# Layer 1's gated MLP: its up projection as a stage of its own with seven block products for eight, and the result through DRAM

## The chip, the cores and the metric

One core of a Trainium2 chip runs the whole program in one launch. The metric is the device time of one execution in microseconds (us). Engines: TensorE (PE; its weight loads are PEld), VectorE (DVE), ScalarE (ACT), GpSimd (POOL) and SyncE (SP), whose queue issues every DMA of this kernel.

## The reference

Two decoder layers over 1024 tokens of width 1024 in float32. Each is attention, a read of a small memory, an output projection added to x, and a gated MLP with a causal convolution, added to x; a final norm follows. The change concerns the MLP of layer 1:

```python
def rmsnorm(x, g):
    y = xf * lax.rsqrt(jnp.mean(xf * xf, axis=-1, keepdims=True) + EPS)
    return (y * g.astype(jnp.float32)).astype(x.dtype)

def conv_glu_ffn(h, w_up, conv_w, conv_b, w_down):      # h = rmsnorm(x, g_ffn): 1024 x 1024
    S = h.shape[1]
    a, b = jnp.split(h @ w_up, 2, axis=-1)              # each 1024 tokens x 2816
    a_pad = jnp.pad(a, ((0, 0), (CONV_WIDTH - 1, 0), (0, 0)))
    a = sum(conv_w[j] * a_pad[:, j:j + S] for j in range(CONV_WIDTH)) + conv_b
    return (jax.nn.silu(a) * b) @ w_down                # back to width 1024
```

## The kernel before

Everything is feature-major: an activation is [feature on partition, token]. The 1024 tokens go in two halves of 512, the width in 8 slices of 128, the inner width of the MLP in NF = 22 tiles of 128. A float32 product x*y runs as three products of rounded parts, H*H + H*L + L*H, where H is the operand rounded and L the rest (`mm3`, lines 209 to 213, so each product is three matmuls, lines 211, 212 and 213). Both operands are needed as such a pair: ScalarE writes H, GpSimd or VectorE subtracts to get L.

Weights stream through the class `Weights` (lines 60 to 113). A first pass over the program records the order of the units; in the second, `_load` (line 77) issues a DMA of a [128, 1024] unit up to `LOAD` = 5 units ahead, and `_split` makes H on ScalarE (line 88) and L on GpSimd (line 89) up to `SPLIT` = 2 units ahead. All big tiles of SBUF come from one pool of 47 buffers of 4 KB a partition (`t4`, line 140). PSUM has two buffers of 1024 columns (`psS`) and four of 512 (`psB`). Engines run in the order in which the program issues. `tick` (line 177) is called with the length of what was just issued on TensorE; background generators (norms, stores) advance by that credit, so they are woven into the issue order by estimated time. A store to DRAM is issued 4000 ns of that clock after it is asked for (`store`, line 160), or as soon as something of the same key is loaded (`flush`).

The MLP is `ffn` (lines 724 to 824). In layer 1 it takes both halves together. For each inner tile f, `up` multiplies the tile of the a-weights with h of both halves (`proj`, 8 slices x 3 matmuls of 512 columns), `conv` multiplies by the norm's scale (line 736), does the three-tap convolution (737 to 744), the activation (745) and the scale for b (746); then come the b-weights, `gate` multiplies (751) and splits the result (755, 756), which stays in SBUF. h here is x * gain, not yet scaled: `gained` (lines 441 to 449) makes it, for the first half as background work and for the second half in a hook of the output projection, and the scale of the tokens (`scale_of`, with the sums of squares in `fold_in`, lines 346 and 354, and `norm_scale`, lines 360 to 388) may come later, but before the first `conv`. After each pair of tiles, `down` multiplies the results of the pair before it with two units of the down weights and adds 128x1024 blocks of PSUM to x (line 802). x of both halves stays in SBUF. The last two pairs go half by half, and the final norm runs behind them.

Ahead of it stand the output projection's last steps (`outs1[1]` in `run`, line 1665, eight steps of `wout_steps`, line 716), beside which the first half's norm runs as background work.

Of the kernel before, what the change touches and what calls it, by code (L numbers as in the profile page):

```python
# [17 lines left out]
F32 = mybir.dt.float32  # L18
# [22 lines left out]
class _Null:  # L41
    """Stands for every object of a pass that only records the weight order."""
# [17 lines left out]
class Weights:  # L60
    """Streams [128, 1024] weight units: load, then split into H and L."""
# [3 lines left out]
    def __init__(self, t, order):  # L65
        self.t, self.order, self.seen = t, order, []
        self.pos = self.loaded = self.ready = 0
        self.ahead = self.LOAD
        self.raw, self.hl = {}, {}

    def _load(self):
        i = self.loaded
        name, idx = self.order[i]
        src = self.t.a[name][idx]
        raw = self.t.t4(1024)
        w = src.shape[-1]
        self.t.nc.sync.dma_start(raw[:, :w], src)
        self.raw[i] = (raw, w)
        self.loaded += 1

    def _split(self):
        i = self.ready
        while self.loaded <= i:
            self._load()
        nc, t = self.t.nc, self.t
        raw, w = self.raw.pop(i)
        hi, lo = t.t4(1024, dt=R32), t.t4(1024, dt=R32)
        nc.scalar.copy(hi[:, :w], raw[:, :w])  # L88
        nc.gpsimd.tensor_tensor(lo[:, :w], raw[:, :w], hi[:, :w].bitcast(F32), op=OP.subtract)  # L89
        self.hl[i] = (hi, lo)  # L90
        self.ready += 1

# [4 lines left out]
    def pump(self):  # L97
        n = len(self.order)
        self.load(min(n, self.pos + self.ahead))
        while self.ready < min(n, self.pos + self.SPLIT):  # L100
            self._split()

    def get(self, name, idx):
        if self.order is None:
            self.seen.append((name, idx))
            return _Null(), _Null()
        i = self.pos
        assert self.order[i] == (name, idx), (self.order[i], name, idx)
# [7 lines left out]
class Unit:  # L116
    """Two generators: the scores with their softmax, and the values."""
# [12 lines left out]
class Trunk:  # L130
# [12 lines left out]
    N_T4 = 47  # L143
# [65 lines left out]
    def mm3(self, out, a, b, start, stop):  # L209
        mm = self.nc.tensor.matmul  # L210
        mm(out, a[0], b[0], start=start, stop=False)  # L211
        mm(out, a[0], b[1], start=False, stop=False)  # L212
        mm(out, a[1], b[0], start=False, stop=stop)  # L213

    def evac_hl(self, hi, lo, src, scale=1.0):
        """hi + lo = scale * src exactly (scale a power of two)."""
# [8 lines left out]
    def split(self, hi, lo, src):  # L225
        """hi + lo = src exactly."""
# [38 lines left out]
    def scratch(self):  # L265
# [11 lines left out]
        self.kB_d = d.tile([2, 256, T], F32, name="kB_d")  # L277

    def rope_tables(self):
        """cos and sin for the 24 frequencies, [frequency, cos|sin, token] in DRAM."""  # L280
# [28 lines left out]
    def load_table(self, kind, hf):  # L309
        """The rows of the table as the rotated rows of a projection need them."""  # L310
# [81 lines left out]
    def norm_apply(self, rb, x, gain, per, out, pace=2500, ease=False):  # L392
        """Generator; appends the split (x * gain) * rb for the tiles [128, per, n] of x."""
# [9 lines left out]
        for i in range(len(x) + 1):  # L403
            if i < len(x):
# [4 lines left out]
                hs.append(h)  # L409
                yield pace  # L410
# [18 lines left out]
    def norm(self, x, gain, out, wait=0, tail=6000, pace=1000, ease=False):  # L429
        """Generator: the whole norm of a half."""  # L430
# [10 lines left out]
    def gained(self, xp, gain, i, out):  # L441
        """Appends the split x * gain of the i-th tile of x, not yet scaled."""
# [8 lines left out]
    def scale_later(self, acc, box, n=HT, wait=5000, big=False):  # L451
        """Generator: the scale of the tokens, put into box."""
# [3 lines left out]
    def scale_of(self, sqs, box, wait=1000):  # L456
        """Generator: the same from the squares of the tiles of x."""
# [8 lines left out]
    def proj(self, out, unit, h, n0=0, n=HT):  # L466
        """out[128 features, n] += unit^T h over the 8 slices of the model width."""
# [8 lines left out]
    def pair(self, name, j0, h, n0=0):  # L476
        """Two feature tiles of a projection, [128, 2, 512 - n0 tokens]."""
# [5 lines left out]
    def rope_store(self, key, S, tab, n0, scale, dst):  # L483
        """(x1 c - x2 s | x2 c + x1 s) * scale of the pair S, split and stored."""
# [15 lines left out]
    def store_hl(self, key, src, dst, scale=1.0, in_sbuf=False):  # L500
        """Splits src [128, 2 tiles, tokens] and stores H and L to dst(hl, tile)."""
# [70 lines left out]
    def mem_norm(self, eng=None):  # L572
        """Generator: the normed memory, split."""
# [56 lines left out]
    def mem_units(self, slot):  # L630
        """The memory read of a half as two pipeline units and the place of its output."""
# [277 lines left out]
    def a_first(self, raw, rb):  # L909
        """The first product runs along with the loads of x."""  # L910
# [25 lines left out]
    def indexer(self, blks):  # L936
        """Generator: the scores of the blocks' queries over all their keys."""
# [285 lines left out]
    def begin_a(self, att):  # L1223
        """Generator: what of attn_a can run before its pipeline."""
# [9 lines left out]
    def run_a(self, hf, att, x, mem, bm, final):  # L1234
        """Runs the attention; returns the last steps of the output projection."""
# [617 lines left out]
```

## Time and profile before

| | us |
|---|---|
| runs | 2714.73, 2715.31, 2716.74 |
| median | 2715.31 |
| the profiled execution: span | 2714.7 |
| of it TensorE busy | 2524.9 |
| VectorE, ScalarE, GpSimd busy | 1649.5, 1137.0, 1289.1 |
| mean granted clock of TensorE | 0.968 |

The span runs from the first to the last instruction of the profiled execution; no other time of that execution is given, and the fastest of the runs, 2714.73 us, is as long as the span to the digit shown. The granted clock is a share of 2.4 GHz; its other level is 1.2 GHz. A matmul's end in these rows is modelled, and matmuls overlap, so the time from start to start is what counts.

### The profile page before, as it was taken

How to read it: one execution, taken by the hardware profiler on the slowest of the kernel's cores; microseconds unless marked ns; L12 is line 12 of the kernel's file. 1: busy time of each engine (PE TensorE's matmuls, PEld its weight loads, DVE VectorE, ACT ScalarE, POOL GpSimd, SP SyncE). 2: the span in 40 equal slices, each digit the busy share in tenths (PEclk: the TensorE clock that was granted, in tenths of full speed). 3: DMA queues.
4: the chain of work that ended last, by engine and by line, in shares of the span. 5: the costliest groups of instructions: out<-in, count | busy, mean ns of one | idle time of the engine just before them, and what ended most of it. 6: DMA issues, size and time to landing. Idle time of an engine off the chain costs nothing.

```text
span 2714.7 us, 33368 instructions
## 1 busy us (share of the span) xinstructions
PE 2524.9 (93%) x12140; PEld 2107.5 (78%) x12140; DVE 1649.5 (61%) x2867; ACT 1137.0 (42%) x2094; POOL 1289.1 (47%) x883
## 2 busy tenths in 40 slices
PE   6788989989998999989999989999999999999997
PEld 5667767867776889878788878888778888888886
DVE  7798997876679466664653453598743333333335
ACT  4344556644542555433332335588622222222223
POOL 4533343345554643345765555566543333333334
PEclk8899999989998999999999999999999999999998
DMA  5444346322222253322332345632211111111101
GB/s 190 152 146 141 117 140 214 128 75 93 87 85 78 68 192 133 109 93 78 109 104 98 111 131 175 232 102 86 78 47 47 47 55 47 47 53 49 47 24 62
DMA packets 105236, 276.10 MB, mean 102 GB/s; under 512 B 11248, under 2 KB 28144, under 8 KB 105072
## 3 DMA queue, kind: packets, MB, share of 16 engines
q1 hardware_dynamic: 105072, 273.98, 30.9%
q8 instruction: 95, 1.56, 0.2%
q14 instruction: 69, 0.57, 0.1%
HBM read 229.89 MB, written 44.04 MB: 101 GB/s over the span
## 4 chain that ended last, share of the span: by engine, by line
PE 47%; DVE 6%; ACT 2%; issue 1%; POOL 1%; DMA 0%; DVEq 0%; ACTq 0%; POOLq 0%
PE pB L211 9%; PE pB L212 9%; PE pB L213 9%; PE pS L211 6%; PE pS L213 6%; PE pS L212 6%; PE pS L1345 1%; PE pB L1399 1%; PE pB L1384 1%; DVE t L739 1%; DVE t L738 1%; DVE t L407 1%; ACT t L88 0%; DVE t L802 0%; DVE t L354 0%
## 5 line engine op out<-in xcount | busy, mean ns | idle before, releaser
L89 POOL TENSOR_TENSOR t<-t,t 128x1024 fp32r<-128x1024 f32 x324 | 792.6, 2462 | 405.4 <-ACT t L88 324.0
L211 PE MATMUL pB<-t,t 128*128 128x512 f32 (+2 forms) x2128 | 800.3, 376 | 7.7 <-DVE t L716 4.1
L212 PE MATMUL pB<-t,t 128*128 128x512 f32 (+2 forms) x2128 | 797.1, 375 | 10.5 <-DVE t L399 8.7
L213 PE MATMUL pB<-t,t 128*128 128x512 f32 (+2 forms) x2128 | 795.7, 374 | 0.1
L211 PE MATMUL pS<-t,t 128*128 128x512 f32 (+1 forms) x1232 | 491.1, 399 | 56.0 <-DVE t L802 31.3
L213 PE MATMUL pS<-t,t 128*128 128x512 f32 (+1 forms) x1232 | 485.0, 394 | 13.5 <-POOL t L89 13.5
L212 PE MATMUL pS<-t,t 128*128 128x512 f32 (+1 forms) x1232 | 484.3, 393 | 1.6 <-DVE t L448 1.6
L212 PEld LDWEIGHTS pB<-t,t 128*128 128x128 f32 (+1 forms) x2128 | 403.6, 190 | 81.9 <-DVE t L399 9.7
L211 PEld LDWEIGHTS pB<-t,t 128*128 128x128 f32 (+1 forms) x2128 | 403.3, 190 | 79.3 <-DVE t L716 5.0
L213 PEld LDWEIGHTS pB<-t,t 128*128 128x128 f32 (+1 forms) x2128 | 403.2, 189 | 72.7 <-POOL t L89 0.7
L746 POOL TENSOR_TENSOR t<-t,t 128x512 f32<-128x512 f32 x88 | 114.3, 1299 | 510.0 <-ACT t L745 503.4
L88 ACT CAST t<-t 128x1024 fp32r<-128x1024 f32 x324 | 328.7, 1043 | 19.4 <-POOL t L89 9.2
L802 DVE TENSOR_TENSOR t<-t,pS 128x1024 f32<-128x1024 f32 (+1 forms) x180 | 214.4, 1195 | 196.3 <-PE pS L213 196.3
L211 PEld LDWEIGHTS pS<-t,t 128*128 128x128 f32 x1232 | 242.4, 197 | 108.7 <-DVE t L802 35.9
L213 PEld LDWEIGHTS pS<-t,t 128*128 128x128 f32 x1232 | 241.8, 196 | 65.9 <-POOL t L89 18.3
L212 PEld LDWEIGHTS pS<-t,t 128*128 128x128 f32 x1232 | 242.8, 197 | 44.7 <-DVE t L448 2.1
L737 ACT ACTIVATE t<-t,conv 128x512 f32<-128x512 f32 x88 | 71.8, 816 | 456.5 <-DVE t L736 456.5
L756 POOL TENSOR_TENSOR t<-t,t 128x512 fp32r<-128x512 f32 x88 | 116.2, 1321 | 182.7 <-ACT t L755 180.4
L220 DVE TENSOR_TENSOR t<-pB,t 128x512 fp32r<-128x512 f32 (+3 forms) x248 | 149.6, 623 | 84.4 <-ACT t L219 78.8
L736 DVE TENSOR_TENSOR t<-pB,t 128x512 f32<-128x512 f32 x88 | 60.7, 690 | 222.4 <-PE pB L213 210.4
L219 ACT CAST t<-pB 128x512 fp32r<-128x512 f32 (+3 forms) x248 | 126.5, 535 | 149.1 <-PE pB L213 81.5
L751 DVE TENSOR_TENSOR t<-t,pB 128x512 f32<-128x512 f32 x88 | 60.4, 687 | 191.9 <-PE pB L213 133.2
(204 smaller groups left out, 2933.3 us busy)
## 6 DMA issues: line engine op xcount, KB each, us to landing
t<-in_up SPq DMA_DIRECT2D x132, 512.0 KB
t<-in_down SPq DMA_DIRECT2D x66, 512.0 KB
t<-in_a_in SPq DMA_DIRECT2D x42, 512.0 KB
t<-in_b_in SPq DMA_DIRECT2D x28, 512.0 KB
t<-in_a_out SPq DMA_DIRECT2D x20, 512.0 KB
t<-in_b_out SPq DMA_DIRECT2D x20, 512.0 KB
t<-in_x SPq DMA_DIRECT2D x16, 512.0 KB
q_d<-t SPq DMA_DIRECT2D x32, 256.0 KB
```

Source lines behind the costliest of these rows:

```text
L88: nc.scalar.copy(hi[:, :w], raw[:, :w])
L89: nc.gpsimd.tensor_tensor(lo[:, :w], raw[:, :w], hi[:, :w].bitcast(F32), op=OP.subtract)
L211: mm(out, a[0], b[0], start=start, stop=False)
L212: mm(out, a[0], b[1], start=False, stop=False)
L213: mm(out, a[1], b[0], start=False, stop=stop)
L219: nc.scalar.copy(hi, src)
L220: nc.vector.tensor_tensor(lo, src, hi.bitcast(F32), op=OP.subtract)
L736: nc.vector.tensor_tensor(v, a, rb[0], op=OP.mult)
L737: nc.scalar.activation(u, v, AF.Identity, bias=cw[:, 3:4], scale=cw[:, 2:3])
L746: nc.gpsimd.tensor_tensor(v, v, rb[0], op=OP.mult)
L756: nc.gpsimd.tensor_tensor(gl[:, f % 2], u, gh[:, f % 2].bitcast(F32), op=OP.subtract)
L802: nc.vector.tensor_tensor(x[dp][:, :, t], x[dp][:, :, t], S, op=OP.add)
```

## The change

The MLP of layer 0 stays. In layer 1, `ffn` is replaced by `ffn_up` and `ffn_down`.

`ffn_up` runs the whole up projection. Tiles f = 0 and 1 go as before, half by half. For f = 2 to 21 the a- and b-weights of a tile are one 2 x 2 block matrix (a or b; first or second 512 of the width), and h is another (first or second 512 of the width; first or second half of the tokens). Their product is formed by seven block products in place of eight (Winograd's variant of Strassen's scheme): seven left factors, of which four are weights as loaded or intermediate sums of them, are made on VectorE from the two raw units (`_factor`), and each is split into H and L of 512 columns; the right factors are h's blocks b11, b21, b22 and four differences of blocks, made and split once, ahead of the first group (`right_factors`). The sums of the products are formed on VectorE and partly in PSUM, where a second product is added to a bank that has been read out already. A product is `product`: 4 slices of `mm3`. The steps that finish one group stand between the products of the next. Since a sum mixes both halves, h is now scaled before the products (`norm_h0`, `norm_h1`), and the scalings in `conv` fall away. h0 is also stored to DRAM and two blocks at a time loaded back for the differences; x of both halves is stored to DRAM.

The gated result is split as before, but stored to DRAM (`G_d`, one [128, 2, 512] tile for each f and half). `ffn_down` loads it, two tiles for each pair and half, one pair ahead (`fetch`), and x is loaded back at the change of stages. Its matmuls and additions are those of `down`. The pool has 51 buffers in place of 47, taken from a smaller DMA scratch (`dynamic_dma_scratch_size=1024`). While the groups run, splits are made four ahead (`AHEAD`). All docstrings and comments are taken out.

```diff
 class Weights:
     def _split(self):
         i = self.ready
-        while self.loaded <= i:
+        while self.loaded < self.need[i]:
             self._load()
...
+        else:
+            src = self._factor(i)
+            hl = t.t4(2, HT, dt=R32)
+            nc.scalar.copy(hl[:, 0], src)
+            nc.gpsimd.tensor_tensor(hl[:, 1], src, hl[:, 0].bitcast(F32), op=OP.subtract)
+            self.hl[i] = (hl[:, 0], hl[:, 1])
         self.ready += 1
+    def _factor(self, i):
+        g, k, tt = self.group, self.order[i][2], self.t.nc.vector.tensor_tensor
...
+        if k == 1:
+            tt(g["s1"][:, 0], b[:, 0], b[:, 1], op=OP.add)
+            tt(g["s1"][:, 1], g["s1"][:, 0], a[:, 0], op=OP.subtract)
+            return g["s1"][:, 1]
+        if k == 2:
+            return g["s1"][:, 0]
+        if k == 3:
+            return a[:, 1]
+        if k == 4:
+            tt(g["s4"][:, 0], a[:, 0], b[:, 0], op=OP.subtract)
+            return g["s4"][:, 0]
+        if k == 5:
+            tt(g["s4"][:, 1], a[:, 1], g["s1"][:, 1], op=OP.subtract)
+            return g["s4"][:, 1]
...
-    N_T4 = 47
+    N_T4 = 51
...
+    def right_factors(self, hf1, out):
...
+        for j in range(2):
+            b11, b21 = self.t4(2, HT), self.t4(2, HT)
+            for i, b in ((j, b11), (2 + j, b21)):
+                self.load("hf", b, self.hf_d[i])
+            while len(hf1) < 3 + j:
+                yield 500
+            yield 2500
...
+            for k, (x, y) in enumerate(((b12, b11), (b22, t[0]), (b22, b12), (b21, t[1]))):
+                tt(t[k], x, y, op=OP.subtract)
+                yield 1400
+                if late:
+                    late()
+                hi, lo = self.t4(2, HT, dt=R32), self.t4(2, HT, dt=R32)
+                nc.scalar.copy(hi, t[k])
+                eng = nc.vector if k % 2 else nc.gpsimd
+                def late(k=k, hi=hi, lo=lo, eng=eng):
+                    eng.tensor_tensor(lo, t[k], hi.bitcast(F32), op=OP.subtract)
+                    out[k].append((hi, lo))
+                yield 1400
...
+    def product(self, out, a, b, start, tick=True):
+        for s in range(4):
+            ks = slice(s * 128, s * 128 + 128)
+            hp = b[s // 2]
+            self.mm3(out, (a[0][:, ks], a[1][:, ks]), (hp[0][:, s % 2], hp[1][:, s % 2]),
+                     start and s == 0, s == 3, again=not start)
+            if s % 2:
+                self.tick(6 * 222)
+    def ffn_up(self, l, h, ready, B, n_std, near_end):
...
+        def keep(f, hf, u):
+            t = self.t4(2, HT, dt=R32)
+            nc.scalar.copy(t[:, 0], u)
+            nc.gpsimd.tensor_tensor(t[:, 1], u, t[:, 0].bitcast(F32), op=OP.subtract)
+            self.store("G", self.G_d[f][hf], t.bitcast(F32))
...
+        def group(f):
+            S, C = self.psS(), self.psB()
+            A, Bk = S[:, :HT], S[:, HT:]
...
+            mul(A, b11, True)
+            nc.scalar.copy(c1, A)
+            yield
+            mul(Bk, B[1], True)
+            tt(u2, c1, Bk, op=OP.add)
+            yield
+            mul(C, B[0], True)
+            tt(v, c1, C, op=OP.add)
+            yield
+            mul(A, b21, False)
+            ua = conv(f, 0, A)
+            yield
+            mul(Bk, B[2], False)
+            tt(c22, v, Bk, op=OP.add)
+            nc.scalar.activation(ua, ua, AF.Silu)
+            yield
+            mul(C, b22, False)
+            tt(c12, u2, C, op=OP.add)
+            ub = conv(f, 1, c12)
+            yield
+            mul(Bk, B[3], False)
+            tt(c21, c1, Bk, op=OP.add)
+            tt(ua, ua, c21, op=OP.mult)
+            nc.scalar.activation(ub, ub, AF.Silu)
+            yield
+            keep(f, 0, ua)
+            tt(ub, ub, c22, op=OP.mult)
+            yield
+            keep(f, 1, ub)
...
+    AHEAD = 4
+    def ffn_down(self, l, xs, G, fetch, hooks, last):
...
+        for c in range(nch - 2):
+            us = weights(c)
+            for hf in range(2):
+                if c + 1 + hf < nch:
+                    fetch(c + 1, hf)
+                down(c, us, G.pop((c, hf)), hf)
...
-        def early_h0():
-            for i in range(4):
-                self.gained(x0[i], g[:, 4], i, h0)
-                yield 3500
+        def norm_h0():
+            yield from self.norm_apply(rb0[0], x0, g[:, 4], 2, h0, 2500, keep=lambda i, t: self.store("hf", self.hf_d[i], t))
+            yield from self.store_x(x0, self.x_d[0])
+            x0.x = None
+        def norm_h1():
+            yield from self.scale_of(sqs, rb1, 1000)
+            del sqs[:]
+            yield from self.norm_apply(rb1[0], x1, g[:, 4], 2, h1, 2000, keep=lambda i, t: hf1.append(t))
+            yield from self.store_x(x1, self.x_d[1])
+            x1.x = None
...
+        b1 = self.add_bg(norm_h1())
+        bT = self.add_bg(self.right_factors(hf1, B))
...
-        self.ffn(1, [(0, x0, h0, rb0, last0), (1, x1, h1, rb1, last1)], last=1)
+        self.ffn_down(1, xs, G, fetch, [last0, last1], 1)
```

## Rows read from the trace of the kernel before

**Rows 1.** The page's busy times: us, share of the span, instructions.
```profile
PE 2524.9 (93%) x12140; PEld 2107.5 (78%) x12140; DVE 1649.5 (61%) x2867; ACT 1137.0 (42%) x2094; POOL 1289.1 (47%) x883
```

**Rows 2.** Windows: each engine's busy us and count, granted clock, DMA share, GB/s.
```profile
core 0: us, PE busy (x) PEld busy (x) DVE busy (x) ACT busy (x) POOL busy (x), PEclk, DMA share, GB/s
0.00:10.00 10.00, 0.62 (x2) 0.50 (x2) 2.21 (x5) 4.22 (x6) 3.08 (x14) 1.00 0.74 239
10.00:20.00 10.00, 7.14 (x23) 4.87 (x22) 9.72 (x14) 8.87 (x11) 4.16 (x2) 1.00 0.76 302
...
1986.00:1992.00 6.00, 6.00 (x19) 4.77 (x20) 1.96 (x12) 0.00 (x0) 0.00 (x0) 0.55 0.21 81
...
2035.00:2470.00 435.00, 435.00 (x1920) 360.18 (x1920) 153.04 (x186) 94.35 (x133) 165.30 (x94) 1.00 0.16 49
```

**Rows 3.** Timeline of TensorE, 1977 to 1988: start, us, instruction, idle before it.
```profile
1978.62 0.39 PE L213 MATMUL pB<-t,t 128*128 128x512 f32 x1
1984.55 1.87 PE L366 MATMUL pS<-ones,t 128*128 128x1 f32 x8 [5.54 <-DVE t L354]
1986.28 0.77 PE L211 MATMUL pB<-t,t 128*128 128x512 f32 x1
1986.86 0.63 PE L212 MATMUL pB<-t,t 128*128 128x512 f32 x1
1987.28 0.63 PE L213 MATMUL pB<-t,t 128*128 128x512 f32 x1
```

**Rows 4.** Groups of instructions, 2035 to 2470: busy us, mean ns, idle before.
```profile
L89 POOL TENSOR_TENSOR t<-t,t 128x1024 fp32r<-128x1024 f32 x41 | 97.9, 2406 | 0.0
...
L756 POOL TENSOR_TENSOR t<-t,t 128x512 fp32r<-128x512 f32 x27 | 34.9, 1292 | 68.8 <-ACT t L755 68.8
...
L738 DVE SCALAR_TENSOR_TENSOR t<-t,conv 128x511 f32<-128x511 f32 x26 | 25.2, 971 | 23.4 <-ACT t L737 23.4
L737 ACT ACTIVATE t<-t,conv 128x512 f32<-128x512 f32 x26 | 21.2, 816 | 187.1 <-DVE t L736 187.1
L739 DVE SCALAR_TENSOR_TENSOR t<-t,conv 128x510 f32<-128x510 f32 x26 | 19.5, 750 | 0.9
L751 DVE TENSOR_TENSOR t<-t,pB 128x512 f32<-128x512 f32 x27 | 18.6, 688 | 86.5 <-PE pB L213 86.5
...
L755 ACT CAST t<-t 128x512 fp32r<-128x512 f32 x27 | 16.7, 620 | 87.4 <-DVE t L751 87.4
L745 ACT ACTIVATE t<-t 128x512 f32<-128x512 f32 x26 | 16.4, 633 | 52.9 <-DVE t L744 32.4 <-DVE t L739 20.6
...
L743 DVE SCALAR_TENSOR_TENSOR t<-prev_a,conv,t 128x1 f32<-128x1 f32 x13 | 2.8, 213 | 0.0
```

**Rows 5.** Line 354: ns shortest/median/longest over the span, then VectorE's timeline at 1983.
```profile
L354 DVE TENSOR_TENSOR t<-t,t x35: 425/1218/3456, 23.5 to 2699.0; 128x1024 f32<-128x1024 f32 x18, 128x512 f32<-128x512 f32 x13, 128x256 f32<-128x256 f32 x4
...
1983.81 0.69 DVE L354 TENSOR_TENSOR t<-t,t 128x512 f32<-128x512 f32 x1
```

**Rows 6.** Timelines of GpSimd and of VectorE, 2023 to 2029.
```profile
2024.54 2.41 POOL L89 TENSOR_TENSOR t<-t,t 128x1024 fp32r<-128x1024 f32 x1
...
2024.82 0.69 DVE L736 TENSOR_TENSOR t<-pB,t 128x512 f32<-128x512 f32 x1 [2.33 <-PE pB L213]
2026.45 1.04 DVE L738 SCALAR_TENSOR_TENSOR t<-t,conv 128x511 f32<-128x511 f32 x1 [0.94 <-ACT t L737]
2027.53 0.75 DVE L739 SCALAR_TENSOR_TENSOR t<-t,conv 128x510 f32<-128x510 f32 x1
```

**Rows 7.** SP's own waits, 2035 to 2470: us in total, times, longest.
```profile
SPq L77 <- POOL t L89: 171.1, 21, 9.5
SPq L77 <- POOL t L756: 112.3, 6, 18.7
```

More of the change, by code (lines that the diff above doesn't have):

```diff
@@ L68, in __init__ @@
         self.ahead = self.LOAD
-        self.raw, self.hl = {}, {}
+        self.raw, self.hl, self.group = {}, {}, {}
+        self.loads, self.need = [], []
+        for e in order or ():
+            if len(e) == 2:
+                self.loads.append(e)
+            elif e[2] < 2:
+                self.loads.append((e[0], e[1][e[2]]))
+            self.need.append(len(self.loads))
     def _load(self):
         i = self.loaded
-        name, idx = self.order[i]
+        name, idx = self.loads[i]
         src = self.t.a[name][idx]
@@ L277, in scratch @@
         self.kB_d = d.tile([2, 256, T], F32, name="kB_d")
+        self.hf_d = [d.tile([128, 2, HT], F32, name=f"hf_d{i}") for i in range(4)]
+        self.G_d = [[d.tile([128, 2, HT], F32, name=f"G_d{f}_{h}") for h in range(2)] for f in range(NF)]
     def rope_tables(self):
@@ L390, with norm_apply @@
     NEWTON = 3500
-    def norm_apply(self, rb, x, gain, per, out, pace=2500, ease=False):
+    def norm_apply(self, rb, x, gain, per, out, pace=2500, ease=False, keep=None):
         nc, hs = self.nc, []
@@ L824, in ffn @@
                     down([c], u, [half])
+    def right_factors(self, hf1, out):
+        nc, tt = self.nc, self.nc.vector.tensor_tensor
+        for k in range(4):
+            out.append([])
+        for j in range(2):
[5 more added lines that the diff above has]
+            yield 2500
+            b12, b22 = hf1[j], hf1[2 + j]
+            t = [self.t4(2, HT) for _ in range(4)]
+            late = None
+            for k, (x, y) in enumerate(((b12, b11), (b22, t[0]), (b22, b12), (b21, t[1]))):
[10 more added lines that the diff above has]
+                yield 1400
+            late()
+            del b11, b21, b12, b22, t, x, y, hi, lo, late
+            hf1[j] = None
@@ new lines, in product, with conv, mul @@
+    def product(self, out, a, b, start, tick=True):
[7 more added lines that the diff above has]
+    def ffn_up(self, l, h, ready, B, n_std, near_end):
+        nc, name = self.nc, f"up{l}"
+        def conv(f, hf, a):
+            cw, prev = self.conv[:, l, f], self.prev_a[:, l, f]
+            u = self.t4(HT)
+            nc.scalar.activation(u, a, AF.Identity, bias=cw[:, 3:4], scale=cw[:, 2:3])
+            nc.vector.scalar_tensor_tensor(u[:, 1:], a[:, :HT - 1], cw[:, 1:2], u[:, 1:], op0=OP.mult, op1=OP.add)
+            nc.vector.scalar_tensor_tensor(u[:, 2:], a[:, :HT - 2], cw[:, 0:1], u[:, 2:], op0=OP.mult, op1=OP.add)
+            if hf == 0:
+                nc.scalar.copy(prev, a[:, HT - 2:])
+            else:
+                nc.vector.scalar_tensor_tensor(u[:, 0:1], prev[:, 1:2], cw[:, 1:2], u[:, 0:1], op0=OP.mult, op1=OP.add)
+                nc.vector.scalar_tensor_tensor(u[:, 0:2], prev, cw[:, 0:1], u[:, 0:2], op0=OP.mult, op1=OP.add)
+            return u
+        def keep(f, hf, u):
[4 more added lines that the diff above has]
+        for hf in range(2):
+            while not ready(hf):
+                self.tick(100)
+            for f in range(n_std):
+                a, b = self.psB(), self.psB()
+                self.proj(a, self.w.get(name, f), h[hf])
+                u = conv(f, hf, a)
+                wb = self.w.get(name, NF + f)
+                if hf and f == n_std - 1:
+                    self.w.SPLIT = self.AHEAD
+                self.proj(b, wb, h[hf])
+                nc.scalar.activation(u, u, AF.Silu)
+                nc.vector.tensor_tensor(u, u, b, op=OP.mult)
+                keep(f, hf, u)
+                del a, b, u, wb
+        b11, b21, b22 = h[0][:2], h[0][2:], h[1][2:]
+        del h[:]
+        while len(B[3]) < 2:
+            self.tick(100)
+        def group(f):
+            S, C = self.psS(), self.psB()
+            A, Bk = S[:, :HT], S[:, HT:]
+            k = [0]
+            def mul(out, b, start):
+                w = self.w.get(name, (f, NF + f), k[0])
+                k[0] += 1
+                self.product(out, w, b, start)
+            tt = nc.vector.tensor_tensor
+            cu, vc, ab = self.t4(2, HT), self.t4(2, HT), self.t4(2, HT)
+            c1, u2, v, c22, c12, c21 = cu[:, 0], cu[:, 1], vc[:, 0], vc[:, 1], ab[:, 0], ab[:, 1]
+            mul(A, b11, True)
[27 more added lines that the diff above has]
+            keep(f, 1, ub)
+        before = iter(())
+        for f in range(n_std, NF):
+            g = group(f)
+            for _ in range(7):
+                next(g)
+                next(before, None)
+            for _ in before:
+                pass
+            before = g
+            near_end(f)
+        for _ in before:
+            pass
+        self.w.SPLIT = Weights.SPLIT
@@ new lines, with down, weights @@
+    AHEAD = 4
+    def ffn_down(self, l, xs, G, fetch, hooks, last):
+        nc, nch = self.nc, NF // 2
+        def down(c, us, g, hf):
+            end = c == nch - 1
+            n = HT // 2 if end and hf == last else HT
+            for q in range(HT // n):
+                t = slice(q * n, q * n + n)
+                for dp in range(4):
+                    S = self.psS().rearrange("p (k t) -> p k t", k=2)[:, :, t]
+                    for e in range(2):
+                        ds = slice((2 * dp + e) * 128, (2 * dp + e) * 128 + 128)
+                        for i, (u, gt) in enumerate(zip(us, g)):
+                            self.mm3(S[:, e], (u[0][:, ds], u[1][:, ds]), (gt[:, 0, t], gt[:, 1, t]), i == 0, i == 1)
+                        self.tick(1280 * n / HT)
+                    xp = xs[hf][dp][:, :, t]
+                    nc.vector.tensor_tensor(xp, xp, S, op=OP.add)
+                    if end:
+                        hooks[hf](2 * dp + 1, q)
+        def weights(c):
+            return [self.w.get(f"down{l}", 2 * c + i) for i in range(2)]
+        for c in range(nch - 2):
+            us = weights(c)
+            for hf in range(2):
+                if c + 1 + hf < nch:
+                    fetch(c + 1, hf)
+                down(c, us, G.pop((c, hf)), hf)
+        us = [weights(c) for c in (nch - 2, nch - 1)]
+        for hf in range(2):
+            fetch(nch - 1, hf)
+        for hf in range(2):
+            for c, u in zip((nch - 2, nch - 1), us):
+                down(c, u, G.pop((c, hf)), hf)
```

74 lines of the change are left out of this document (55 added, 19 removed).

## The prediction, written before the changed kernel ran

> **What bounds the kernel now.** I read the page's busy times first: TensorE is busy for 2524.9 of 2714.7 us, VectorE for 61%, GpSimd for 47% [rows 1]. A share over the whole span does not say what layer 1's gated MLP waits for, so I then cut the windows there [rows 2]. From 2035 to 2470 us TensorE shows 435.00 us busy in 435.00, 1920 matmuls at a granted clock of 1.00 (2.4 GHz): 435.00 / 1920 = 0.2266 us for one, and no gap. This stage ends when its matmuls are done; a matmul taken out there is worth 0.2266 us, as long as nothing else becomes late. The timeline of TensorE shows the one place ahead of it where the stage waits [rows 3]: after the matmul at 1978.62 nothing starts until 1984.55, 5.5 us idle for VectorE's sum of squares (line 354), and after it the matmuls run 0.43 us apart, at the granted clock of 0.55 of the window 1986 to 1992 [rows 2]. That is 5.93 - 0.23 = 5.7 us of waiting and about 13 matmuls at 0.20 us more each, 2.6 us: 8.3 us in all. The groups of instructions give durations and show who has room [rows 4]; two timelines show how VectorE and GpSimd hinder each other [rows 6].
>
> The profiled span is 2714.7 us, the median of the runs 2715.3: I work on the span and add the 0.6 us at the end.
>
> **Part 1: seven products for eight.** One inner tile f costs today 2 weight tiles x 2 halves x 8 slices x 3 = 96 matmuls. A product of the new scheme is 4 slices x 3 = 12 matmuls of the same shape, and there are seven: 84. For 20 of the 22 tiles (n_std = 2 stay as they are) this takes away 20 x 12 = 240 matmuls: 240 x 0.2266 = 54.4 us. A group then lasts 84 x 0.2266 = 19.03 us on TensorE, where a tile had 21.75. The down projection keeps its 96 matmuls for a pair of tiles.
>
> **Part 2: what a group asks of the other engines, in 19.03 us.** GpSimd: seven half-wide weight splits and two of the result. The row for this shape is line 756, 1.292 us [rows 4]; 9 x 1.29 = 11.6. ScalarE: seven casts and two more at 0.62, one copy out of PSUM at about that, two activations at 0.82 and two at 0.63: 9.1 us. VectorE: four sums of weights of 512 columns at 0.69 [rows 5], five sums with PSUM at 0.69 (line 751), four convolution steps at 0.75, two small ones at 0.21, two gating products at 0.69 [rows 4]: 2.8 + 3.4 + 3.0 + 0.4 + 1.4 = 11.0 us. Each by itself fits.
>
> VectorE and GpSimd don't run freely side by side. At 2026.45 VectorE's line 738, both of its inputs in SBUF, takes 1.04 us and ends 0.54 us after GpSimd's subtraction (2024.54 + 2.41 = 2026.95); the next, line 739, with GpSimd idle, takes 0.75. Line 736, which reads PSUM, takes 0.69 although GpSimd runs [rows 6]. So a VectorE step with two SBUF inputs waits for the GpSimd step in progress, and one with a PSUM input does not. Of the 11.0 us, the four weight sums, the second half's two convolution steps, the two gating products and the two small ones are of the first kind: 2.8 + 1.5 + 1.4 + 0.4 = 6.1 us. One after the other with GpSimd's 11.6 that is 17.7 of 19.03 us: it fits, with little room.
>
> The tightest place is the middle accumulator: the fifth product's sum must be read out by VectorE before the seventh product adds to the same bank, and between the two lies only the sixth, 2.72 us. Ahead of that read on VectorE stand the convolution of the fourth product (0.82 on ScalarE, then 2 x 0.75) and two weight sums of the next group (2 x 0.69); with the read, 0.69, it is 4.4 us from the end of the fourth product, and 2 x 2.72 = 5.44 are available. One collision with GpSimd (at most 1.29) makes it late by 0.3 us. Bounds: 0, and 20 x 1.3 = 26 us where every group has the worst; I take 3 us, near the lower end, because in the trace line 738 loses 0.22 us on average (0.971 against 0.750) and line 739 nothing [rows 4].
>
> **Part 3: the start of the stage.** Before the first group there are the two plain tiles, 4 x 2 x 24 x 0.2266 = 43.5 us on TensorE as today. Beside them now stands much more: the second half's norm must be applied before the products (today it is applied behind them), and eight differences of the right factors are made and split. GpSimd: six unit splits at 2.41 (two are made ahead), four result splits, two low parts of h1 and four of the factors at 2.41, and four half splits for the first group: 14.5 + 5.2 + 4.8 + 9.6 + 5.2 = 39.3 us. VectorE, with two SBUF inputs: the sum of squares, 2 x 1.22 + 3 x 0.69 = 4.5 (median and timeline of line 354, [rows 5]); eight applications of the scale at 0.75, 6.0; two low parts, eight differences and four low parts at 1.22, 17.1: 27.6 us. Together 66.9 us, against TensorE's 43.5.
>
> Taken one after the other, that is 23 us too much. But rows 6 show that 0.2 us of such a VectorE step pass beside GpSimd (0.54 of 0.75): 25 x 0.2 = 5 us less; and the last two factors of the second pair are wanted only by the fifth and seventh product, 10.9 and 16.3 us later: another 6 us. I take 12 us of waiting and 2.6 us of half clock behind it, 14.6, in place of today's 8.3: +6.3 us. Bounds: +0 us of waiting, if all fits (-8.3), and 23 + 5 (+20).
>
> The Trainium skill (page "SBUF — State Buffer", section "Who interferes with whom") says that the shared pair of ports is an exclusive lock held for the whole instruction; by that rule the 5 us would not be saved, and the start would stand at 2676 in place of 2671. The row with 0.54 us speaks against "the whole instruction"; it bears out the lock itself.
>
> Ahead of it, under the last 20.8 us of the output projection, the first half's norm now takes the place of two scalings (the same eight VectorE steps, four casts more on ScalarE, two low parts on each engine in place of none); VectorE is busy there for the two halves' scaling already, and loses the second half's. I cost this at nothing; if h0 is late, TensorE waits for it at 1959, by at most the 3 us that one tile's steps take.
>
> **Part 4: through DRAM.** 44 tiles of 0.524 MB are stored and loaded. In the up stage a group loads 1.05 MB and stores 1.05 MB in 19 us, 110 GB/s; in the down stage a pair of tiles loads 2 weights and 4 results, 3.15 MB in 21.75 us: 145 GB/s. Today's stretch moves 49, but the first 20 us of the kernel moved 239 and 302 GB/s [rows 2]: hidden, at 0. SP issues all of it in order: a store waits for its split, and weight loads queue behind it. They are five units ahead, 2.5 groups or 48 us; the longest wait of such a load today is 18.7 us [rows 7]. If this cover failed, each group would wait for its own load. At the change to the down stage x0 (2.1 MB, 7 to 9 us at those rates) is asked for behind the last group's issue and x1 behind it; the first sum into x is 2.7 us into the stage, and two PSUM buffers give 5.4. I take 1 us (0 to 9). The down stage is then 11 x 21.75 us as now, and the final norm's tail is unchanged.
>
> **Sum.** 2714.7 - 54.4 + 3 + 6.3 + 1 = 2670.6; with 0.6 around it, 2671 us. Four more buffers can move the waits of earlier stages by some us either way; I have no row for that.
>
> **The rivals.**
> A. *All of the start hides.* The waits behind the differences end before the first group wants them. For it: the factors are spread over 26 us. Against it: 66.9 us of mutually exclusive work. 2671 - 14.6 - 3 = 2653.
> B. *The groups are paced by VectorE and GpSimd in part*, 20.5 us each in place of 19.03: 17.7 of 19.03 us leaves 7% for handing over. 20 x 1.5 = 29, less the 3 counted: 2697.
> C. *Slower: every two-input step of VectorE in a group waits for a whole GpSimd step.* Then VectorE needs 11.0 + 10 x 1.29 = 23.9 us for a group: 20 x (23.9 - 19.03) = 97 us more, 2765. It delays TensorE from a mean wait of 0.80 us on (11.0 + 10 x 0.80 = 19.0), and the kernel is slower than before from 1.03 us on (a group of 21.3). For it: GpSimd's share rises from 38% (165.3 of 435) to 61%. Against it: the mean wait is 0.22 us at 38%, and the longest wait is one step, now 1.29 and not 2.41.
> D. *The DRAM path shows.* One exposed load at each change (fill of the down stage, x0 and x1, first result tiles), 15 to 25 us: 2690. Against it: the rates above.
> E. *The seven products are not what runs* (other counts of matmuls): the diff has 12 in a product and seven calls, so nothing for it.
>
> **How the numbers follow.** Forecast 0.57 (2658 to 2685), A 0.13, B 0.14, C 0.06, D 0.10. The range goes from 2652 (A) to 2700 (B), which leaves out C and the tails of B and D. Apart from no change a measurement of this kernel tells 0.2%, 5.4 us: faster by more 0.91, within it 0.03, slower 0.06 (C).
>
> **What would show it.** In the up stage windows of 19.0 us with 84 matmuls and TensorE at 1.00; matmuls in all 240 fewer; GpSimd near 60% there; in the start, idle time of TensorE released by the factor lines or by weight splits, 10 to 15 us, with a clock near 0.5 behind it; between the fifth and the seventh product no gap over 0.3 us on average; SP's waits not passed on to TensorE. I am wrong if a group takes over 20 us, if the gaps lie in the down stage, or if the start loses under 5 or over 25 us.

## The result and the profile after

The changed kernel takes 2818.53 us (median of 4 runs, 2814.77 to 2822.33) against 2715.48 for the kernel before: a ratio of 1.0378, 95% interval 1.0363 to 1.0392. It is 103 us slower where 44 us faster was forecast, and 118 us above the range. The profiled execution took 2818.82 us, its span is 2817.0.

The page's busy times first, the counterpart of [rows 1]:

```profile
PE 2511.8 (89%) x11900; PEld 2079.7 (74%) x11900; DVE 1786.1 (63%) x3019; ACT 1190.2 (42%) x2218; POOL 1363.3 (48%) x951
```

TensorE has 240 matmuls fewer, as counted (12140 to 11900), but only 13 us less busy time, and its share falls from 93% to 89%. The windows tell where; they are the plain tiles, the first group, the other 19 groups, and the down stage (span, each engine's busy us and count, granted clock, DMA share, GB/s):

```profile
1959.00:2023.00 64.00, 51.55 (x202) 39.89 (x201) 56.16 (x51) 28.30 (x35) 42.10 (x16) 0.87 0.54 194
2023.00:2063.00 40.00, 22.94 (x87) 17.76 (x86) 21.65 (x22) 12.84 (x21) 20.67 (x14) 0.79 0.27 92
2063.00:2550.00 487.00, 394.32 (x1598) 311.68 (x1597) 215.40 (x323) 158.52 (x285) 226.27 (x171) 0.95 0.26 93
2550.00:2784.00 234.00, 233.11 (x1045) 193.19 (x1043) 109.94 (x94) 30.05 (x34) 61.32 (x39) 1.00 0.35 133
```

The down stage is as forecast: TensorE is busy in 233.11 of 234 us beside 133 GB/s. The 19 groups take 487 us, 25.6 each; before, the stretch of [rows 2] had no idle time at all. VectorE is busy there 215 and GpSimd 226 of 487 us: neither is short of time. What TensorE waits for in these 19 groups is a list of two lines (us in total, times, longest):

```profile
PE pS L256 <- ACT prev_a L933: 50.0, 19, 2.6
PE pS L256 <- ACT t L979: 42.7, 19, 2.3
```

Line 256 is the first matmul of `mm3`; line 979 is `nc.scalar.copy(c1, A)`, the copy of accumulator A behind the first product; line 933 is the last of the convolution's reads of A behind the fourth. Each stands once in every group. One group shows who waits: TensorE, ScalarE and VectorE around a fifth product (start, us, instruction, idle before it):

```profile
2154.72 0.39 PE L258 MATMUL pS<-t,t 128*128 128x512 f32 x1
2157.73 0.50 PE L256 MATMUL pS<-t,t 128*128 128x512 f32 x1 [2.63 <-ACT prev_a L933]
...
2155.14 0.78 ACT L929 ACTIVATE t<-pS,conv 128x512 f32<-128x512 f32 x1 [5.96 <-PE pS L258]
2157.52 0.16 ACT L933 COPY prev_a<-pS 128x2 f32<-128x2 f32 x1 [1.60 <-DVE t L931]
...
2155.95 0.75 DVE L930 SCALAR_TENSOR_TENSOR t<-pS,conv,t 128x511 f32<-128x511 f32 x1 [2.84 <-ACT t L929]
2156.74 0.75 DVE L931 SCALAR_TENSOR_TENSOR t<-pS,conv,t 128x510 f32<-128x510 f32 x1
```

The last matmul of the fourth product starts at 2154.72 and is done when its first reader starts, at 2155.14. The four readers follow one another (0.78, 0.75, 0.75, 0.16), and only behind the last, at 2157.73, does the fifth product begin. But the fifth product writes Bk, not A. A and Bk are columns 0 to 511 and 512 to 1023 of one PSUM tile: `A, Bk = S[:, :HT], S[:, HT:]`. Nothing that the readers read is touched by the product that waits for them.

### The profile page after: what moved, and what is told of

Its sections match the earlier page's. It is cut to its first block, busy times and chain, and to the rows that moved or that the text cites. A ratio compares the mean times of both kernels' runs of the same rounds, so it can differ in the third digit from the quotient of the medians.

```text
span 2817.0 us, 33672 instructions
## 1 busy us (share of the span) xinstructions
PE 2511.8 (89%) x11900; PEld 2079.7 (74%) x11900; DVE 1786.1 (63%) x3019; ACT 1190.2 (42%) x2218; POOL 1363.3 (48%) x951
## 5 line engine op out<-in xcount | busy, mean ns | idle before, releaser
L100 POOL TENSOR_TENSOR t<-t,t 128x1024 fp32r<-128x1024 f32 (+1 forms) x288 | 712.4, 2489 | 485.0 <-ACT t L99 340.9
L256 PE MATMUL pS<-t,t 128*128 128x512 f32 (+1 forms) x1632 | 659.7, 404 | 168.5 <-ACT t L979 57.1
L258 PE MATMUL pS<-t,t 128*128 128x512 f32 (+1 forms) x1632 | 649.2, 398 | 12.9 <-POOL t L100 12.9
L257 PE MATMUL pS<-t,t 128*128 128x512 f32 (+1 forms) x1632 | 649.4, 398 | 1.6 <-DVE t L498 1.6
L256 PE MATMUL pB<-t,t 128*128 128x512 f32 (+1 forms) x1648 | 617.0, 374 | 10.8 <-DVE t L766 4.6
L257 PE MATMUL pB<-t,t 128*128 128x512 f32 (+1 forms) x1648 | 613.9, 373 | 14.0 <-POOL t L447 6.8
L258 PE MATMUL pB<-t,t 128*128 128x512 f32 (+1 forms) x1648 | 611.8, 371 | 0.7 <-POOL t L100 0.7
L256 PEld LDWEIGHTS pS<-t,t 128*128 128x128 f32 x1632 | 321.0, 197 | 254.0 <-ACT t L979 65.6
L258 PEld LDWEIGHTS pS<-t,t 128*128 128x128 f32 x1632 | 321.9, 197 | 83.4 <-POOL t L100 17.6
L257 PEld LDWEIGHTS pS<-t,t 128*128 128x128 f32 x1632 | 322.2, 197 | 60.1 <-DVE t L498 2.0
L257 PEld LDWEIGHTS pB<-t,t 128*128 128x128 f32 x1648 | 315.3, 191 | 69.1 <-POOL t L447 9.0
L256 PEld LDWEIGHTS pB<-t,t 128*128 128x128 f32 x1648 | 315.9, 192 | 65.9 <-ACT t L466 5.9
L258 PEld LDWEIGHTS pB<-t,t 128*128 128x128 f32 x1648 | 314.6, 191 | 55.1 <-POOL t L100 1.8
L99 ACT CAST t<-t 128x1024 fp32r<-128x1024 f32 (+1 forms) x288 | 292.5, 1043 | 101.6 <-PE pS L258 44.4
L106 POOL TENSOR_TENSOR t<-t,t 128x512 fp32r<-128x512 f32 x140 | 187.1, 1349 | 268.1 <-ACT t L105 268.1
L1042 DVE TENSOR_TENSOR t<-t,pS 128x1024 f32<-128x1024 f32 (+1 forms) x92 | 108.0, 1174 | 125.1 <-PE pS L258 124.4
L852 DVE TENSOR_TENSOR t<-t,pS 128x1024 f32<-128x1024 f32 x88 | 106.4, 1217 | 63.6 <-PE pS L258 63.4
L1198 DVE SCALAR_TENSOR_TENSOR t<-t,wtok,t 128x384 f32<-128x384 f32 (+5 forms) x90 | 109.6, 1218 | 7.8 <-ACT t L1193 4.0
```

The lines of the kernel that those rows point to most:

```text
L106: nc.gpsimd.tensor_tensor(hl[:, 1], src, hl[:, 0].bitcast(F32), op=OP.subtract)
L256: mm(out, a[0], b[0], start=start, stop=False, skip_group_check=again)
L257: mm(out, a[0], b[1], start=False, stop=False, skip_group_check=again)
L258: mm(out, a[1], b[0], start=False, stop=stop, skip_group_check=again)
L852: nc.vector.tensor_tensor(x[dp][:, :, t], x[dp][:, :, t], S, op=OP.add)
L1042: nc.vector.tensor_tensor(xp, xp, S, op=OP.add)
```

## The experiments

### Theories

T: the wait between a write and the reads before it is set for a whole PSUM tile, so that products into one half wait for the readers of the other. L: VectorE and GpSimd hinder each other so much that the readers come late (my rival C). P: the products wait for their own operands. For the start of the stage, X: VectorE and GpSimd take turns on work with two SBUF inputs, and the sum of it is longer than the plain tiles; Q: the queue of one engine alone is the bound.

### Three tiles for three accumulators

```diff
-            S, C = self.psS(), self.psB()
-            A, Bk = S[:, :HT], S[:, HT:]
+            A, Bk, C = self.psB(), self.psB(), self.psS()[:, :HT]
```

> One edit: accumulators A and Bk, which share one 1024-column PSUM tile after the change, get a 512-column tile each; C takes half of a 1024-column tile that nothing else uses. Theory T (a wait is set for a whole PSUM tile, so the second product waits for the copy of A and the fifth for the convolution's reads of A, although both write Bk): both waits vanish, a group falls from 24.5 to 27.7 us to 19.0 to 19.6 us, the granted clock of the groups' stretch goes to 1.00, and 2818 loses 20 x (2.4 + 2.8) = 104 and some 28 us of half clock behind the gaps: about 2686 (2675 to 2700; the long first gap near 2026 us stays, for its factors are late by themselves). Rival L (VectorE and GpSimd, hindering each other, are what makes A's readers late, and the next reader takes over): gaps move to the seventh product or to the weight splits, groups stay over 22 us, 2740 or more. Rival P (the second and fifth product are held by their own operands): nothing changes, 2818.

Measured: 2687.01 us, ratio to the kernel before 0.9891 (0.9876 to 0.9906). The windows of this kernel, in the same order of stages:

```profile
1962.00:2026.00 64.00, 49.98 (x205) 38.72 (x205) 56.42 (x52) 28.07 (x35) 41.82 (x16) 0.92 0.55 196
2026.00:2059.00 33.00, 23.56 (x83) 17.26 (x82) 21.32 (x22) 13.12 (x21) 20.85 (x15) 0.84 0.31 112
2059.00:2421.00 362.00, 362.00 (x1599) 299.75 (x1598) 213.90 (x322) 158.73 (x285) 226.54 (x171) 1.00 0.34 117
2421.00:2660.00 239.00, 235.29 (x1057) 194.89 (x1056) 115.07 (x97) 31.75 (x38) 65.48 (x41) 1.00 0.39 147
```

The 19 groups now lie in a window of 362.00 us with 362.00 busy, 19.04 each, at a clock of 1.00. VectorE and GpSimd do the same work as in the changed kernel (213.90 and 226.54 us against 215.40 and 226.27). T holds to within a microsecond; L and P fall. It also divides the 125 us that the 19 groups lose: 92.7 us are the two waits, and in the other 394.32 - 362.00 = 32.3 us matmuls count as busy for longer. Not all of this is the clock. The timeline of the changed kernel shows, behind a wait (start, us, instruction, idle before it):

```profile
2079.31 0.50 PE L256 MATMUL pS<-t,t 128*128 128x512 f32 x1 [2.63 <-ACT prev_a L933]
...
2080.59 0.41 PE L258 MATMUL pS<-t,t 128*128 128x512 f32 x1
2080.82 0.62 PE L256 MATMUL pS<-t,t 128*128 128x512 f32 x1
2081.23 0.63 PE L257 MATMUL pS<-t,t 128*128 128x512 f32 x1
```

From 2080.82 on the matmuls start 0.43 us apart, the pace of 1.2 GHz, for 3 us. Counted over the whole window, this happens behind 13 of the 38 waits, with 99 matmuls: 99 x 0.20 = 20 us. The other 12 us stand at the edges of the waits, where the last matmul ahead of one counts for its full 0.39 us and the first behind it takes longer. The next experiment has such edges without the half clock.

### Another pair in one tile

```diff
-            S, C = self.psS(), self.psB()
-            A, Bk = S[:, :HT], S[:, HT:]
+            A, S = self.psB(), self.psS()
+            Bk, C = S[:, :HT], S[:, HT:]
```

> A gets a 512-column tile of its own, and Bk and C become the two halves of one 1024-column tile. Same arithmetic, same banks' worth of PSUM. Theory T: no wait ahead of the second and the fifth product any more; instead the third product (writes C) waits for the read of Bk behind the second (one VectorE step, about 0.9 us), the sixth for the read of Bk behind the fifth (about 1 to 2 us, since the convolution's steps and two weight sums stand before it on VectorE), the seventh for the read of C behind the sixth (about 0.9 us): groups of 22 to 23.5 us, 2745 to 2790. If the waits belonged to the places of the products or to the hardware's banks, they would stay ahead of the second and fifth product (2818) or be gone as in the kernel with three tiles (about 2686).

Measured: 2770.9 us (one run). The waits of TensorE in groups 1 to 19:

```profile
PE pS L256 <- ACT t L105: 32.3, 18, 1.8
PE pS L256 <- DVE t L995: 17.8, 19, 0.9
PE pS L256 <- DVE t L982: 15.9, 19, 0.8
PE pS L256 <- ACT t L99: 0.9, 1, 0.9
```

The waits have moved to where T puts them: 0.8 us ahead of the third product for the read of Bk (line 982), 1.8 ahead of the sixth, 0.9 ahead of the seventh for the read of C (line 995); none ahead of the second and fifth. The middle one is named after a weight cast, line 105, which by the order of issue is the next group's; in the group at 2131 the read of Bk (line 991) ended at 2147.63 and the sixth product began at 2147.78, so the name alone would mislead here. A group takes 23.4 us, and the clock stays at 1.00 (window 2061 to 2505):

```profile
2061.00:2505.00 444.00, 377.06 (x1596) 294.87 (x1595) 213.35 (x323) 158.67 (x285) 226.47 (x171) 1.00 0.28 100
```

Although no matmul runs at half clock here, TensorE is busy for 15 us more than the 362.00 us of the kernel with three tiles: 0.26 us for each of the 57 waits. At that price the 38 waits of the changed kernel account for 10 of its 32.3 us.

### The third pair

```diff
+            Bk, S = self.psB(), self.psS()
+            A, C = S[:, :HT], S[:, HT:]
```

> As the changed kernel, but A and C are the halves of the shared tile and Bk has its own. Theory T: only the fourth product (writes A) waits, for the read of C behind the third, one VectorE step, 0.9 to 1.1 us; the third would wait for the copy of A, which is done under the second, and the sixth for the convolution's reads of A, 2.5 us, which the fifth covers (2.7) or nearly. Groups of 19.9 to 20.5 us; 2687 + 20 x 1.1 = 2709 (2703 to 2717). If sharing a tile did not matter, 2687.

Measured: 2711.86 us (one run); the wait in groups 1 to 19:

```profile
PE pS L256 <- DVE t L985: 14.8, 19, 0.8
```

One wait remains, ahead of the fourth product, for the read of C; groups of 20.3 us. So the same arithmetic takes 2818, 2771, 2712 or 2687 us, by which accumulators share a tile and how soon one's reads are followed by the other's writes. That the tile is the unit is shown; what sets it, the framework that places the semaphores or something below it, was not separated.

### The start: three plain tiles

```diff
-        self.ffn_up(1, hs, lambda hf: len((h0, h1)[hf]) == 4, B, 2, near_end)
+        self.ffn_up(1, hs, lambda hf: len((h0, h1)[hf]) == 4, B, 3, near_end)
```

(on top of the three tiles)

> The three separate accumulators, and three plain tiles ahead of the groups in place of two. Theory for the start (VectorE and GpSimd take turns on work with two SBUF inputs, some 67 us or more of it, while the plain tiles give TensorE only 43.5 us): with 65.3 us of plain tiles the gap of 14 us ahead of the first group's second product goes, and most of the 5.9 us gap for the second half's norm; that costs 12 matmuls, 2.7 us, and gives some 15 us: about 2671 where the kernel with two plain tiles is at 2686. Rival (the gap belongs to the chain through ScalarE's queue of the first group, not to the amount of work): the gap only moves 22 us later, and the time is 2.7 us above the other's.

Measured: 2682.55 us, 0.9878 (0.9862 to 0.9895), against 2687.01. The gaps of the first group are gone (its seven products take 19.0 us), so the rival falls; but the plain tiles took 92.7 us for 65.3 of matmuls, a loss of 27, where it had been 20.6, so the gain was not 15 but 4.5, and the two intervals overlap. The list of waits in the plain tiles now begins with GpSimd's splits of weight units (line 100), which took 1.4 us in the base:

```profile
PE pB L258 <- POOL t L100: 9.5, 4, 4.8
```

More plain tiles bring more weight splits along.

### The start: less for GpSimd

```diff
-                eng = nc.vector if k % 2 else nc.gpsimd
+                eng = nc.vector
...
-            eng = nc.gpsimd if i % 2 else nc.vector
+            eng = low or (nc.gpsimd if i % 2 else nc.vector)
...
-            yield from self.norm_apply(rb1[0], x1, g[:, 4], 2, h1, 2000, keep=lambda i, t: hf1.append(t))
+            yield from self.norm_apply(rb1[0], x1, g[:, 4], 2, h1, 2000, keep=lambda i, t: hf1.append(t), low=nc.vector)
```

> Base: three separate accumulators, two plain tiles (2687). Edit: the two low parts of h1 and the four of the right factors that GpSimd makes (2.4 us each alone) go to VectorE (1.22 each alone). In the base VectorE shows 29.1 us busy and GpSimd 26.2 of the 31 us from 1995 to 2026, and TensorE loses about 35 us between the start of the plain tiles and the second group. Theory X (the two engines take turns, so the sum of their work counts): the sum falls by 6 x 1.2 = 7 us, and the kernel becomes some 7 us faster, 2680 (2676 to 2683). Rival Q (VectorE's own queue is the bound): its queue grows by 6 x 1.22 = 7 us and the kernel becomes that much slower, 2694.

Measured: 2683.41 us, 0.9872 (0.9856 to 0.9889). Q's 2694 (a ratio of 0.991) is outside. The median is 3.6 us lower, as X's direction has it, but the interval overlaps that of the base (0.9876 to 0.9906), so the step is not clear of the noise. Then the weight splits of the plain tiles as well:

```diff
+        self.w.eng = nc.vector
...
-                    self.w.SPLIT = self.AHEAD
+                    self.w.SPLIT, self.w.eng = self.AHEAD, nc.gpsimd
```

> As the last one, and also the low parts of the plain tiles' weight units (six in the stage and some behind them, 2.4 us each on GpSimd) go to VectorE, until the last plain product. Theory X: another 6 x 1.2 = 7 us less in the sum, about 2672 (2666 to 2680). Rival Q: VectorE has another 7 us to do, slower than the last one: 2700. A middle way: VectorE, now with nearly all of the work (about 60 us against 43.5 of TensorE), becomes the bound by itself; then the step from the last kernel to this one is near zero.

Measured: 2682.71 us, 0.9869 (0.9855 to 0.9884): no step that can be told from zero, the middle way. With three plain tiles:

> As the last one, with three plain tiles: 65.3 us of plain products over about 67 us of VectorE's work. Theory X: nearly no gap ahead of the groups, 12 matmuls (2.7 us) more; 35 us of loss shrink to about 10: 2687 - 25 + 3 = 2665 (2658 to 2672). Rival Q: as with three plain tiles and GpSimd's share of the work, 2683 or more.

Measured: 2679.45 us (2676.81 to 2682.27), 0.9859 (0.9844 to 0.9874). With the next one this is the fastest version that leaves nothing out, 1.4% below the kernel before. X had hoped for 2665, which is outside the interval; Q's 2683 (0.987) is inside. Its windows, plain tiles and groups:

```profile
1959.00:2047.00 88.00, 73.25 (x299) 55.96 (x299) 67.52 (x88) 39.58 (x50) 12.54 (x8) 0.96 0.52 186
2047.00:2409.00 362.00, 362.00 (x1598) 299.75 (x1598) 210.31 (x316) 159.38 (x287) 227.69 (x172) 1.00 0.33 119
```

GpSimd is almost idle in the plain tiles (12.54 of 88 us) and VectorE not full (67.52), yet they lose 22 us: 14.75 idle, the rest in matmuls that take longer at a clock of 0.96. The longest entries among the waits of the plain tiles:

```profile
PE pB L257 <- ACT t L100: 5.4, 3, 2.1
PE pS L414 <- DVE t L402: 3.0, 1, 3.0
PE pB L259 <- DVE t L101: 2.3, 4, 0.8
```

These are the weight casts on ScalarE (line 100), the splits behind them on VectorE (101) and the sum of squares (402). So what remains looks like chains of steps ahead of single products rather than the amount of work; no run took a single chain away. Two more edits on it changed nothing:

> As the last one, and the two low parts of h0 that GpSimd makes go to VectorE as well. In the base the plain tiles begin with four gaps of about 1 us each for them. Theory X: 2 to 4 us less than the last one, since each is 1.2 us shorter and no longer behind a weight split of 2.4 us. Rival Q: the sum of squares behind them on VectorE comes 2.4 us later, and the gap for it grows: no change or 2 us more.

Measured: 2679.42 us. The gaps at the first product shrank and the one for the sum of squares grew, as Q says (3.0 us to 4.1 for the latter).

> VectorE making the low parts in the plain tiles, as in the kernel at 2679.5 with three of them, but with four plain tiles. With three there is no gap left in the first group, and each plain tile costs 2.7 us: expected 2679.5 + 2.7 = 2682. Only if the gaps of about 1 to 2 us between the second half's plain tiles are still the differences' overhang does it win: 2676.

Measured: 2682.32 us, 0.9873 (0.9858 to 0.9888).

### The start: no differences

```diff
-        bT = self.add_bg(self.right_factors(hf1, B))
+        bT = self.add_bg(self.right_factors(hf1, h1, B))
...
+        while len(h1) < 4:
+            yield 500
+        for k in range(4):
+            out[k].extend(h1[:2])
```

> Base: three separate accumulators, two plain tiles (2687). Left out: the four differences of h's blocks and their splits, and the loads for them; the first two tiles of h1 stand in for all four right factors. All products, norms, weight splits and stores stay. Theory X (the differences are what the plain tiles cannot cover): the 14.4 us over a normal group in the first group go, and of the 9 us over 21.8 us in the second half's plain tiles all but 3: 2687 - 14 - 6 = 2667 (2662 to 2670). Rival W (the second half's norm and the weight splits of 2.4 us on GpSimd hold the plain tiles, the differences come after): only the first group's part goes, 2673 to 2677. Rival Q (ScalarE's order of issue): 2683 or more.

Measured: 2672.80 us, 0.9835 (0.9818 to 0.9851), 14.2 us less than with the differences. Its windows, plain tiles and first group:

```profile
1963.00:2026.00 63.00, 50.18 (x203) 39.07 (x204) 39.45 (x50) 24.57 (x32) 32.06 (x15) 0.92 0.57 200
2026.00:2045.00 19.00, 19.00 (x85) 15.75 (x84) 7.95 (x12) 8.52 (x16) 12.94 (x11) 1.00 0.24 84
```

The first group takes 19.0 us in place of 33.5: all of the 14.2. The plain tiles stay at 63 us, 20 above their matmuls: 13 idle, and the rest in matmuls that take longer at a clock of 0.92. The longest waits among them:

```profile
PE pB L257 <- POOL t L447: 4.9, 2, 4.3
PE pB L256 <- ACT t L466: 2.7, 2, 1.9
PE pS L413 <- DVE t L401: 2.6, 1, 2.6
```

Lines 466 and 447 are the casts and low parts of h, line 401 is the sum of squares. So it went as W has it: the differences cost the first group's gaps, and the plain tiles wait for the norms and the splits.

## Why the prediction was wrong, step by step

**The step that failed: the accumulators of a group (part 2).** I wrote that the tightest place is the read of the fifth product's sum before the seventh "adds to the same bank", and took the other accumulators as free of each other, although the diff shows A and Bk cut from one tile. The kernel before could not warn in its trace: there both halves of such a tile are filled first and read after, so no write ever stood behind a read of the other half. With A and Bk in one tile, the second product waits for the copy of A (42.7 / 19 = 2.3 us) and the fifth for the four reads of A (2.6 us). Each of these writes comes right behind the reads' own product, so there is no slack at all, where I had counted on one product between a sum and the next write to its bank. My sum had 3 us for all the waits of the groups, and nothing for these two; they took 92.7 us in 19 groups. The three pairings show the mechanism, and separate tiles give back 131.5 us: 2818.5 to 2687.0.

**Its second half: the clock.** I had priced half clock only at the start. The matmuls of the 19 groups take 32 us more: about 20 of them at half clock, behind 13 of the 38 waits of 2.3 and 2.6 us, and about 12 at the edges of the waits. Behind the three waits of 0.8 to 1.8 us in a group of the second pairing the clock stayed at 1.00, and only the edges were left. So a wait is not priced by its own length alone.

**Seven products (part 1): right.** 240 matmuls, 54.4 us: with separate tiles a group takes 19.04 us, forecast 19.03.

**VectorE and GpSimd in the groups (part 2): right, and with room.** Forecast 11.0 us on VectorE and 11.6 on GpSimd; the windows give 213.9 / 19 = 11.3 and 226.5 / 19 = 11.9. The read ahead of the seventh product never made it wait: 0 for my 3 us. The collisions with GpSimd do occur, and are larger than the 0.22 us that I had taken from line 738: with separate tiles, line 931 on inputs in SBUF takes 1.66 us in the mean, and 0.75 where it reads PSUM. But VectorE has the room, so they cost nothing, and B and C are refuted by the 362.00 of 362 us. C's price of 2765 was nearer than my forecast, but for a reason that did not occur.

**The start (part 3): right in kind, too small.** I took 14.6 us of loss, and called myself wrong above 25. With separate tiles, the plain tiles take 64.1 us for 43.5 of matmuls and the first group 33.5 for 19.0: 35 us. Two timelines of that kernel, VectorE and GpSimd, show the turns that I had summed (the counterpart of [rows 6]):

```profile
1999.14 2.69 DVE L447 TENSOR_TENSOR t<-t,t 128x1024 fp32r<-128x1024 f32 x1 [0.61 <-ACT t L466]
2001.75 3.35 DVE L894 TENSOR_TENSOR t<-t,t 128x1024 f32<-128x1024 f32 x1
...
2000.71 6.64 POOL L447 TENSOR_TENSOR t<-t,t 128x1024 fp32r<-128x1024 f32 x2
2009.55 3.37 POOL L100 TENSOR_TENSOR t<-t,t 128x1024 fp32r<-128x1024 f32 x1
```

A step of 1.22 us on VectorE takes 3.35 and one of 2.4 on GpSimd 3.3 to 3.4: each contains most of the other's. The Trainium skill (page "SBUF — State Buffer", section "SBUF: two separate sides") has the shared pair of ports locked for the whole instruction; these rows agree with the lock. A pair takes 3.35 us and not 1.22 + 2.4 = 3.6, though, so some 0.3 us of it still pass side by side, as I had read from [rows 6]. The 5 us that I subtracted for this were therefore not the fault; without them the sum would have been nearer to 35 us by luck. The sum was not the whole: without the differences, 20 us remained, and moving steps away from GpSimd gave some 4 us, hardly clear of the noise, where the sum promised 14. What I had left out, by the waits listed with the last experiment, is that the second half's norm is a chain (sums of squares, scale, four tiles, two splits) whose end the first product of that half needs at once, and that a product then waits for single splits behind it.

**DRAM (part 4): right.** The down stage with separate tiles has 235.29 us busy of 239 at 147 GB/s (forecast 145); at the change of stages TensorE is idle once, for 1.7 us ahead of the first sums into x, forecast 1. VectorE shows why (start, us, instruction):

```profile
2425.86 0.69 DVE L999 TENSOR_TENSOR t<-t,t 128x512 f32<-128x512 f32 x1
2426.47 0.68 DVE L1003 TENSOR_TENSOR t<-t,t 128x512 f32<-128x512 f32 x1
2427.07 2.34 DVE L1041 TENSOR_TENSOR t<-t,pS 128x1024 f32<-128x1024 f32 x2
```

It goes from the last group's steps to these sums (line 1041) without a pause, so the wait is for its own queue and not for a load. The other gap in this window, 2.0 us at 2657.92, stands in the last pairs and has its counterpart in the kernel before (at 2683.81). Rival D is refuted.

With the start's 35 us for 14.6, and nothing for the groups, the sum would have been 2714.7 - 54.4 - 8.3 + 35 + 2 = 2689, the span of the kernel with separate tiles (2688.9). The start's term was mis-sized by 20 us; the shared tile is the rest.

## What to carry to other kernels

For every accumulator, write down the tile it is cut from, and for each write the last read of any part of that tile: two accumulators that are read at different times belong in different tiles, even when their columns don't touch. Where an engine's rows of a new stage cannot be seen in the trace of before, the order of writes and reads in one period is to be listed from the code, per tile, before any durations are added. A wait in every period can cost more than its length: at its edges (0.26 us each in the second pairing), and by the clock behind it, which fell behind some waits of 2.3 and 2.6 us and behind none of 1.8 or less in these groups.

## What the runs showed that was not expected

The clock: with two gaps of 2.3 and 2.6 us in each group of 25.6 us, matmuls ran at half clock for 3 us behind 13 of 38 gaps, 20 us in all, and the mean granted clock was 0.95; three shorter gaps in each 23.4 us, 3.5 us together, left it at 1.00. And four readers of one accumulator, on two engines, follow one another: the 0.16 us copy of two columns (line 933) starts 0.78 us after VectorE's step on the same accumulator began, when that step is done, though both only read. It does so too where A has a tile of its own (second pairing: start 2145.74, 1.60 us idle for line 931); what makes it wait was not separated.
